# Another opening for a two-layer transformer kernel: norm weights in PSUM, a written order for the first token tiles, transpositions in idle time

## The chip, the cores and the metric

The kernel runs on one core of a Trainium2 chip. A core has TensorE (matrix products, into PSUM; PE in the profile), VectorE (DVE), ScalarE (ACT), GpSimd (POOL) and SyncE (SP, which issues most transfers). The engines run side by side; each works through its own list of instructions in order and waits on semaphores for the others. The metric is the time of one execution on the device in microseconds (us), lower is better; several executions are taken and their median is given.

## What is computed

A trunk of two layers over 1024 tokens of width 1024, all in float32: differential attention in the first, latent attention in the second, a gated MLP with a short convolution behind each. The change lies in the first steps of the first layer:

```python
def rms_norm(x, g):
    y = x * lax.rsqrt(jnp.mean(x * x, axis=-1, keepdims=True) + NORM_EPS)
    return y * g

h = rms_norm(x, attn_norm_g[0])
qkv = h @ w_qkv                      # 1024 x 3072: 8 heads, each 128 columns of q, k and v
q, k, v = jnp.split(qkv, 3, axis=-1) # then a partial rotary embedding of q and k
```

## The kernel before

**Tokens and heads.** The 1024 tokens are eight tiles of 128 rows; tiles 0 to 3 are half 0, tiles 4 to 7 half 1. A product on TensorE wants the features on the partitions, so each normalized tile is transposed ("turned") by eight 128x128 products with the identity matrix `ident`, four into each of two PSUM banks of 512 columns. Every product of the model is done in three: a float32 number is split into a high part (rounded to the format that TensorE takes at full rate, float32r) and a low part (the rest), and `mm3` adds high x low, high x high and low x high. ACT writes high parts (`hi`, line 141, CAST in the profile), DVE or POOL low parts (`lo`, line 144).

**A token tile** (`token_tile`): ACT squares the tile and sums (`squares`, line 171), DVE scales the sum (176), POOL takes the power -1/2 (177), DVE multiplies the tile by the root and by the norm weights `g` (328), TensorE turns it (196), ACT and DVE split it into `H`. The norm weights are loaded once with each row repeated on all 128 partitions (`gain`, line 203, a tile of 512 KB in s11).

**A unit** (`da_unit`) is one projection of one head for one half: (head, which, half) with which 0 for q, 1 for k, 2 for v. It is 24 products of 512 columns into PSUM bank `u`, of which there is one. For q and k the rotary embedding follows (`rope`: DVE 247 and 248 read the bank, POOL 249 and 250 combine), then ACT, DVE or POOL write the parts. For v, ACT copies the bank, and the result is turned. PSUM has two double banks `S`, three banks `b` and one `u`; names are handed out in rotation, and whoever gets one waits until its last reader is done.

**Order.** Code is written once for all engines. Unless a manual schedule is open, a scheduler in the framework orders each engine's list by its own estimate of times; inside `manual_schedule` the order of the code stands. The first part of `diff_attention` (lines 340 to 360) is left to the scheduler: weights of head 0 are fetched and split (`fetch_w`, `split_w`; the raw weights have two places in turn), tiles 0 to 3, unit (0,1,0), unit (0,0,0), tiles 4 to 7, unit (0,2,0). After that the loop over heads is played from a list (`DA_ORDER`), which neither kernel changes; it begins with scores of head 0 and unit (0,1,1). In the profile's names the letter is the kind of place: s, u and h are SBUF pieces of 2048, 1024 and 512 columns when they are 128 rows of data, and `b`, `u` and `S` written by TensorE are PSUM.

## Time and profile before

| | us |
|---|---|
| runs: 3, median | 2438.91 |
| lowest, highest | 2438.78, 2440.64 |
| the profiled execution's own time | 2438.93 |
| its span, first to last instruction | 2437.1 |

The profiled execution's time is 1.83 us more than its span, for what lies around the first and last instruction. How to read the lines below: a row of the order of time has the start and the length in us, engine, line of the kernel, operation, tile written <- tiles read, and in square brackets how long the engine had been idle and what ended that. A row that groups instructions has their number, busy time in us, mean of one in ns. A row of a window has its bounds, its length, the busy time (with number of instructions) of TensorE, its weight loads, DVE, ACT and POOL, the granted TensorE clock (1.00 is full), the share of the DMA engines and GB/s. Ends of products are modelled: two that follow each other overlap, so the distance of starts is what one costs.

### The profile page before, as it was taken

To read this page: it belongs to the slowest core of one execution; us is meant where nothing else is said; L and a number is where in the kernel's file an instruction comes from. 1 tells how busy PE (TensorE), PEld (TensorE's weight loads), DVE (VectorE), ACT (ScalarE), POOL (GpSimd) and SP (SyncE) were. 2 spreads that over 40 slices of the span, in tenths; PEclk is the share of its full clock that TensorE was granted. 3 is DMA by queue.
4 is the path that set the end of the run, shared out by engine and by line. 5 is a ranking of instruction groups with operands and counts; after the bars stand their busy time and mean duration, and the time that the engine had idled before them with its cause. 6 is when DMAs were issued, how large, how long until landed. Compare 5 with 4: busy or idle time off the path is not lost.

```text
span 2437.1 us, 32476 instructions
## 1 busy us (share of the span) xinstructions
PE 2361.4 (97%) x11864; PEld 1995.5 (82%) x11864; DVE 1916.4 (79%) x3108; ACT 1299.4 (53%) x2417; POOL 639.8 (26%) x502
## 2 busy tenths in 40 slices
PE   7999999899999999999999999999989999999998
PEld 5888888777888888878889888888878888887886
DVE  6577777847988888899965888886488888888997
ACT  5677777845444444444444777775354444443443
POOL 5555544525100000000042566655340000000001
PEclk9999999999999999999999999999999999999999
DMA  4111111313222222554231211124222222227501
GB/s 153 43 47 36 35 36 44 130 57 114 78 93 80 78 87 79 185 181 134 68 104 52 77 49 31 49 63 130 91 87 87 79 93 80 78 87 276 173 1 78
DMA packets 95135, 214.68 MB, mean 88 GB/s; under 512 B 8640, under 2 KB 33856, under 8 KB 94784
## 3 DMA queue, kind: packets, MB, share of 16 engines
q1 hardware_dynamic: 86080, 185.35, 22.9%
q10 hardware_dynamic: 8896, 27.27, 3.0%
q8 instruction: 93, 1.52, 0.3%
q14 instruction: 66, 0.54, 0.1%
HBM read 160.15 MB, written 52.43 MB: 87 GB/s over the span
## 4 chain that ended last, share of the span: by engine, by line
PE 75%; DVE 10%; ACT 5%; DMA 3%; issue 3%; POOL 3%; SPq 0%; POOLq 0%; ACTq 0%; DVEq 0%
PE S L133 12%; PE S L135 12%; PE S L134 12%; PE b L135 8%; PE b L134 8%; PE b L133 8%; PE u L133 3%; PE u L134 3%; PE u L135 3%; PE b L259 3%; DVE s L144 2%; ACT u L141 1%; PE u L1572 1%; PE u L1571 1%; POOL s L144 1%
## 5 line engine op out<-in xcount | busy, mean ns | idle before, releaser
L177 POOL TENSOR_TENSOR st<-st,mhalf 128x1 f32<-128x1 f32 x56 | 33.9, 606 | 1327.5 <-DVE st L176 1327.5
L141 ACT CAST u<-h 128x512 fp32r<-128x512 f32 (+1 forms) x242 | 145.9, 619 | 296.1 <-DVE h L669 263.5
L133 PE MATMUL S<-s,u 128*128 128x512 f32 (+1 forms) x752 | 286.5, 381 | 7.7 <-DVE s L144 5.6
L135 PE MATMUL S<-s,u 128*128 128x512 f32 (+1 forms) x752 | 285.2, 379 | 0.0
L134 PE MATMUL S<-s,u 128*128 128x512 f32 (+1 forms) x752 | 285.1, 379 | 0.0
L133 PE MATMUL b<-s,u 128*128 128x512 f32 x588 | 230.5, 392 | 1.2 <-ACT u L141 1.2
L135 PE MATMUL b<-s,u 128*128 128x512 f32 x588 | 229.6, 391 | 0.0
L134 PE MATMUL b<-s,u 128*128 128x512 f32 x588 | 229.3, 390 | 0.0
L717 DVE SCALAR_TENSOR_TENSOR u<-u,conv,u 128x1023 f32<-128x1023 f32 (+1 forms) x176 | 224.7, 1277 | 1.4 <-ACT u L713 1.4
L163 POOL TENSOR_TENSOR u<-u,st 128x384 f32<-128x384 f32 (+7 forms) x160 | 170.9, 1080 | 156.4 <-DVE st L1555 92.8
L133 PE MATMUL u<-s,s 128*128 128x512 f32 x448 | 181.4, 405 | 9.4 <-DVE h L248 6.9
L141 ACT CAST s<-u 128x512 fp32r<-128x512 f32 (+2 forms) x204 | 131.7, 682 | 105.9 <-PE u L135 34.7
L144 DVE TENSOR_TENSOR u<-b,u 128x512 fp32r<-128x512 f32 (+1 forms) x256 | 157.4, 629 | 27.0 <-ACT u L141 25.8
L135 PE MATMUL u<-s,s 128*128 128x512 f32 x448 | 176.7, 394 | 0.0
L134 PE MATMUL u<-s,s 128*128 128x512 f32 x448 | 176.4, 394 | 0.0
L133 PEld LDWEIGHTS S<-s,u 128*128 128x128 f32 x752 | 142.5, 189 | 36.4 <-DVE s L144 6.4
L134 PEld LDWEIGHTS S<-s,u 128*128 128x128 f32 x752 | 142.6, 190 | 26.3
L135 PEld LDWEIGHTS S<-s,u 128*128 128x128 f32 x752 | 142.5, 190 | 26.1
L720 ACT ACTIVATE u<-u 128x1024 f32<-128x1024 f32 x44 | 46.7, 1062 | 195.8 <-DVE u L717 195.8
L141 ACT CAST u<-b 128x512 fp32r<-128x512 f32 (+1 forms) x256 | 133.6, 549 | 25.7 <-PE b L259 13.0
L141 ACT CAST s<-h 128x512 fp32r<-128x512 f32 x144 | 86.6, 619 | 111.7 <-DVE h L900 51.0
L144 DVE TENSOR_TENSOR s<-u,s 128x512 fp32r<-128x512 f32 (+1 forms) x182 | 129.1, 743 | 10.4 <-ACT s L141 10.3
(261 smaller groups left out, 6617.4 us busy)
## 6 DMA issues: line engine op xcount, KB each, us to landing
u<-in_ffn_up SPq DMA_DIRECT2D x88, 512.0 KB, 3.6
g_d<-u ACTq DMA_DIRECT2D x44, 512.0 KB, 2.6
u<-in_ffn_down SPq DMA_DIRECT2D x66, 256.0 KB, 5.3
u<-g_d SPq DMA_DIRECT2D x62, 256.0 KB, 4.6
s<-in_da_wqkv SPq DMA_DIRECT2D x24, 512.0 KB, 3.7
x_d<-u SPq DMA_DIRECT2D x16, 512.0 KB, 2.6
s<-x_d SPq DMA_DIRECT2D x8, 1024.0 KB, 8.9
u<-o_d SPq DMA_DIRECT2D x24, 256.0 KB, 2.8
```

Of the source, the lines that this page charges most:

```text
L133: mm(out, lh, rl, start=first, stop=False, skip_group_check=onto)
L134: mm(out, lh, rh, start=False, stop=False, skip_group_check=onto)
L135: mm(out, ll, rh, start=False, stop=last, skip_group_check=onto)
L141: self.nc.scalar.copy(out, src)
L144: (eng or self.nc.vector).tensor_sub(out, src, hi.bitcast(F32))
L163: self.nc.gpsimd.tensor_mul(x, x, s.to_broadcast(list(x.shape)))
L177: nc.gpsimd.tensor_tensor(r, s, self.mhalf, ALU.pow)
L259: self.nc.tensor.transpose(ps[:, j * P : (j + 1) * P], probs[t][:, k : k + P], self.ident)
L717: nc.vector.scalar_tensor_tensor(t[half][:, back:], u[half][:, : S - back], w, t[half][:, back:], ALU.mult, ALU.add)
L720: nc.scalar.activation(t[0], t[0], AF.Silu)
L1571: nc.tensor.matmul(o[:, c0:], v, al, start=kb == 0, stop=False)
L1572: nc.tensor.matmul(o[:, c0:], v, ah, start=False, stop=kb == 2 * p + 1)
```

## The change

It has five parts, all before the loop over heads.

1. **Norm weights** (`gain_bank`). Instead of 128 repeated rows, 8 rows of 128 numbers are loaded (4 KB). TensorE turns them into a 128x8 column block, DVE widens each column to 128 equal columns (in s11), and TensorE turns these eight blocks into a double bank S, which then holds the weights on every partition. The tiles' norms read them from there; the bank is held until tile 7 is normalized.
2. **A written order** for tiles 0 to 3 on TensorE, DVE, ACT and POOL (`first_tiles`), and for TensorE alone up to the end of the products of unit (0,2,0). The scaling of the sum of squares moves from DVE to POOL for tiles 0 to 4. The squares' output, which nobody reads, goes to u13 instead of a double bank S.
3. **Idle transpositions** (`fill`): 5, 6, 14, 3, 4 and 10 products with `ident` whose results are overwritten, each group ahead of work that waits for another engine.
4. **The first unit's high products first** (`late`): eight high x high, then eight low x high, then eight high x low, so that the low parts are wanted last.
5. **Places**: unit (0,0,0) accumulates in a bank b; tile 4 is turned ahead of it, tile 5 behind it, tile 6 in the middle of unit (0,2,0), tile 7 behind its products. Tiles x0 to x4 are fetched at the start, x5 to x7 at once when their places are free; the fetches of head 1's weights and of the constants are written later.

```diff
+    def gain_bank(self, place, rows, src):
+        rows, wide = self.at(rows, [KD, P]), self.at(place, [P, KD, P])
+        self.nc.sync.dma_start(rows, src.rearrange("(k p) -> k p", p=P))
+        def make():
+            ps = self.bank("u")
+            self.fill(ps, self.ident, 5)
+            self.nc.tensor.transpose(ps[:, :KD], rows, self.ident[:KD, :KD])
+            self.nc.vector.tensor_copy(wide, ps[:, :KD].unsqueeze(2).to_broadcast([P, KD, P]))
+            g = self.big()
+            self.fill(g, self.ident, 6)
+            for k in range(KD):
+                self.nc.tensor.transpose(g[:, k * P : (k + 1) * P], wide[:, k, :], self.ident)
+            return g
+        return make
+
+    def fill(self, ps, src, n):
+        for _ in range(n):
+            self.nc.tensor.transpose(ps[:, :P], src[:, :P], self.ident)
...
-            r = self.rstd(x, self.big(), D)
+            r = r4 if i == 4 else self.rstd(x, junk, D)
...
-        xs = [fetch_x(0)]
-        g = self.gain("s11", a["attn_norm_g"][0])
-        xs += [fetch_x(1), fetch_x(2)]
+        def first_tiles():
+            E = mybir.EngineType
+            order = self.tc.manual_schedule(engines={E.PE, E.DVE, E.Activation, E.Pool})
+            order.__enter__()
...
+            def root(i):
+                s[i] = self.squares(xs[i], junk)
+                r[i] = self.stat()
+                nc.gpsimd.tensor_scalar(s[i], s[i], 1.0 / D, EPS, ALU.mult, ALU.add)
+                nc.gpsimd.tensor_tensor(r[i], s[i], self.mhalf, ALU.pow)
+
+            def norm(i):
+                nc.vector.scalar_tensor_tensor(xs[i], xs[i], r[i], g, ALU.mult, ALU.mult)
+
+            def turn(i, banks, n):
+                self.fill(banks[0], xs[i - 1] if i else self.ident, n)
+                for kg, ps in enumerate(banks):
+                    for k in range(4):
+                        b = kg * 512 + k * P
+                        nc.tensor.transpose(ps[:, k * P : (k + 1) * P], xs[i][:, b : b + P], self.ident)
...
+            g = gain()
+            for i in range(3):
+                root(i)
+                norm(i)
+            turn(0, (self.bank(), self.bank()), 14)
+            high(0)
+            root(3)
+            turn(1, (self.bank(), self.bank("u")), 3)
+            high(1)
+            low(0)
+            norm(3)
+            for b in (slice(0, 512), slice(512, D)):
+                self.hi(w[:, 0, b], raw[:, b])
+            for b in (slice(0, 512), slice(512, D)):
+                self.lo(w[:, 1, b], raw[:, b], w[:, 0, b], nc.gpsimd)
+            turn(2, both(self.big()), 4)
+            high(2)
+            low(1)
+            low(2)
+            turn(3, (self.bank(), self.bank()), 10)
+            high(3)
+            root(4)
+            low(3)
+            order.__exit__(None, None, None)
+            return g, r[4]
+
+        gain = self.gain_bank("s11", "h4", a["attn_norm_g"][0])
+        xs = [fetch_x(i) for i in range(4)]
+        junk = self.at("u13", [P, D])
         fetch_w(0, 1)
-        xs += [fetch_x(3)]
+        xs += [fetch_x(4)]
+        g, r4 = first_tiles()
+        nc.sync.dma_start(tab, a["rope_da"])
         fetch_w(0, 0)
-        nc.sync.dma_start(tab, a["rope_da"])
-        split_w(0, 1)
-        for i in range(4):
-            token_tile(i, xs[i])
-            if i == 1:
-                self.load_constants()
-        xs += [fetch_x(4), fetch_x(5), fetch_x(6)]
+        xs += [fetch_x(5), fetch_x(6), fetch_x(7)]
         fetch_w(0, 2)
+        order = self.tc.manual_schedule(engines={mybir.EngineType.PE})
+        order.__enter__()
         split_w(0, 0)
-        self.run([unit(0, 1, 0)])
+        self.run([unit(0, 1, 0, True)])
+        token_tile(4, xs[4])
+        self.run([unit(0, 0, 0, False, "b")])
+        token_tile(5, xs[5])
         split_w(0, 2)
+        last = [unit(0, 2, 0)]
+        self.run(last, 2)
+        token_tile(6, xs[6])
+        self.run(last, 1)
+        token_tile(7, xs[7])
+        order.__exit__(None, None, None)
+        self.run(last)
         fetch_w(1, 1)
-        self.run([unit(0, 0, 0)])
-        for i in range(4, NT):
-            if i + 3 < NT:
-                xs += [fetch_x(i + 3)]
-            token_tile(i, xs[i])
-        self.run([unit(0, 2, 0)])
+        self.load_constants()
...
-    def da_unit(self, R, H, W, which, half, hd, tab):
+    def da_unit(self, R, H, W, which, half, hd, tab, late=False, bank="u"):
...
+            if late:
+                nc.tensor.matmul(acc, part(0, k), tok(0, k), start=k == 0, stop=False)
+                continue
...
+        for w, p in ((1, 0), (0, 1)) if late else ():
+            for k in range(KD):
+                nc.tensor.matmul(acc, part(w, k), tok(p, k), start=False, stop=p == 1 and k == KD - 1)
```

What stands in the engines' lists. TensorE before, from its first instruction (`b` and `u` on the left of the arrow are banks, u_59 to u_63 tiles x0 to x3; L196 is the turn of a tile, L133 to L135 the three products of `mm3`):

```order
L196 MATMUL b_178<-ident,u_59_155 128x128 x4
L196 MATMUL b_185<-ident,u_59_155 128x128 x4
L196 MATMUL b_199<-ident,u_61_159 128x128 x4
L196 MATMUL b_206<-ident,u_61_159 128x128 x4
L196 MATMUL b_235<-ident,u_62_161 128x128 x4
L196 MATMUL b_242<-ident,u_62_161 128x128 x4
L196 MATMUL b_256<-ident,u_63_164 128x128 x4
L196 MATMUL b_263<-ident,u_63_164 128x128 x4
L133 MATMUL u_280<-s_49_141,s_64_168 128x512
L134 MATMUL u_280<-s_45_137,s_64_168 128x512
L135 MATMUL u_280<-s_45_137,s_64_168 128x512
```

TensorE now, from the turn of tile 1 on (L226 is `fill`, L382 the turn of a tile, L519 and L526 the first unit; u_62 to u_64 are x1 to x3, s_45 and s_46 the high parts of half 0):

```order
L226 MATMUL b_245<-ident,u_61_158 128x128 x3
L382 MATMUL b_245<-ident,u_62_160 128x128 x4
L382 MATMUL u_246<-ident,u_62_160 128x128 x4
L226 MATMUL S_267<-ident,u_62_160 128x128 x4
L382 MATMUL S_267<-ident,u_63_162 128x128 x8
L226 MATMUL b_286<-ident,u_63_162 128x128 x10
L382 MATMUL b_286<-ident,u_64_164 128x128 x4
L382 MATMUL b_287<-ident,u_64_164 128x128 x4
L519 MATMUL u_330<-s_45_137,s_67_172 128x512 x4
L519 MATMUL u_330<-s_46_138,s_67_172 128x512 x4
L526 MATMUL u_330<-s_45_137,s_67_172 128x512 x4
L526 MATMUL u_330<-s_46_138,s_67_172 128x512 x4
```

Behind each tile's turn there is now a group of fills for the next tile's bank, and the first unit begins with eight products that need high parts only. ACT before, from its third instruction on (L171 squares, L141 high parts; s_64 and s_91 are weights):

```order
L171 ACTIVATE S_192,st_71_193<-u_61_159 128x1024
L141 CAST s_45_137<-b_178 128x4x128
L171 ACTIVATE S_228,st_79_229<-u_62_161 128x1024
L141 CAST s_46_138<-b_185 128x4x128
L141 CAST s_64_168<-s_54_146 128x1024
L141 CAST s_45_137<-b_199 128x4x128
L171 ACTIVATE S_249,st_84_250<-u_63_164 128x1024
L141 CAST s_46_138<-b_206 128x4x128
L141 CAST s_91_277<-s_54_146 128x1024
```

ACT now, from its third instruction on:

```order
L171 ACTIVATE u_65_166,st_72_202<-u_62_160 128x1024
L171 ACTIVATE u_65_166,st_74_208<-u_63_162 128x1024
L141 CAST s_45_137<-b_214 128x4x128
L141 CAST s_46_138<-b_215 128x4x128
L171 ACTIVATE u_65_166,st_78_240<-u_64_164 128x1024
L141 CAST s_45_137<-b_245 128x4x128
L141 CAST s_46_138<-u_246 128x4x128
L141 CAST s_67_172<-s_54_146 128x512 x2
L141 CAST s_45_137<-S_267 128x4x128
L141 CAST s_46_138<-S_267 128x4x128
L141 CAST s_45_137<-b_286 128x4x128
L141 CAST s_46_138<-b_287 128x4x128
```

Three squares now come first, the fourth ahead of tile 1's high parts, and the weights' high part (in two halves) behind these. POOL before, from the fourth tile's root on (L177 is a root, L249 and L250 the rope, s_91, s_96 and s_126 low parts of weights):

```order
L177 TENSOR_TENSOR st_85_252<-st_84_250,mhalf 128x1
L144 TENSOR_TENSOR s_91_277<-s_54_146,s_91_277 128x1024
L177 TENSOR_TENSOR st_104_363<-st_103_361,mhalf 128x1
L177 TENSOR_TENSOR st_109_384<-st_108_382,mhalf 128x1
L177 TENSOR_TENSOR st_114_405<-st_113_403,mhalf 128x1
L144 TENSOR_TENSOR s_96_316<-s_54_146,s_96_316 128x1024
L177 TENSOR_TENSOR st_119_426<-st_118_424,mhalf 128x1
L249 TENSOR_TENSOR h_94_306<-h_94_306,s_53_145 128x512
L250 TENSOR_TENSOR h_93_305<-h_93_305,h_94_306 128x512
L144 TENSOR_TENSOR s_126_479<-s_54_146,s_126_479 128x1024
L249 TENSOR_TENSOR h_99_346<-h_99_346,s_53_145 128x512
L250 TENSOR_TENSOR h_98_345<-h_98_345,h_99_346 128x512
```

POOL now, over the same work (L270 and L271 are the rope, s_90 the query weights, s_105 the value weights, s_121 head 1's key weights):

```order
L144 TENSOR_TENSOR s_90_327<-s_54_146,s_90_327 128x1024
L177 TENSOR_TENSOR st_102_421<-st_101_419,mhalf 128x1
L270 TENSOR_TENSOR h_93_356<-h_93_356,s_53_145 128x512
L177 TENSOR_TENSOR st_108_457<-st_107_455,mhalf 128x1
L271 TENSOR_TENSOR h_92_355<-h_92_355,h_93_356 128x512
L144 TENSOR_TENSOR s_105_439<-s_54_146,s_105_439 128x1024
L177 TENSOR_TENSOR st_112_483<-st_111_481,mhalf 128x1
L144 TENSOR_TENSOR s_121_534<-s_54_146,s_121_534 128x1024
L270 TENSOR_TENSOR h_99_407<-h_99_407,s_53_145 128x512
L271 TENSOR_TENSOR h_98_406<-h_98_406,h_99_407 128x512
```

The rope of k now stands ahead of the low part of the value weights, and both that and the low part of head 1's key weights stand ahead of the rope of q, where before only the latter did. On SP the fetch of the 8 rows is first, then x0 to x3, key weights, x4, the rotary table, query weights, lambda, constants, x5 to x7, value weights, head 1's key weights.

More of the change, by code (lines that the diff above doesn't have):

```diff
@@ L419 @@
     )
-    def da_unit(self, R, H, W, which, half, hd, tab):
+    def da_unit(self, R, H, W, which, half, hd, tab, late=False, bank="u"):
         nc = self.nc
-        acc = self.bank("u")
+        acc = self.bank(bank)
+        part = lambda w, k: W[w][:, k * P : (k + 1) * P]
+        tok = lambda p, k: H[p][half][k // 4][:, k % 4, :]
         for k in range(KD):
-            wh, wl = (w[:, k * P : (k + 1) * P] for w in W)
-            rh, rl = (H[part][half][k // 4][:, k % 4, :] for part in range(2))
-            self.mm3(acc, wh, wl, rh, rl, k == 0, k == KD - 1)
+            if late:
+                nc.tensor.matmul(acc, part(0, k), tok(0, k), start=k == 0, stop=False)
+                continue
+            self.mm3(acc, part(0, k), part(1, k), tok(0, k), tok(1, k), k == 0, k == KD - 1)
             if k in (1, 3, 5):
                 yield
+        for w, p in ((1, 0), (0, 1)) if late else ():
+            for k in range(KD):
+                nc.tensor.matmul(acc, part(w, k), tok(p, k), start=False, stop=p == 1 and k == KD - 1)
         if which == 2:
```

18 lines of the change are left out of this document (16 added, 2 removed).

## The prediction

> **What bounds the kernel now.** I read the page first, then the start in order of time, then the clock.
>
> ```profile
> PE 2361.4 (97%) x11864; PEld 1995.5 (82%) x11864; DVE 1916.4 (79%) x3108; ACT 1299.4 (53%) x2417; POOL 639.8 (26%) x502
> PE 75%; DVE 10%; ACT 5%; DMA 3%; issue 3%; POOL 3%; SPq 0%; POOLq 0%; ACTq 0%; DVEq 0%
> ```
>
> TensorE is busy 97% of the span and three quarters of the chain that ended last; the edit touches only the first 50 us, so the question is how early TensorE gets through them. The stage in order of time (all engines up to 24 us, TensorE alone below):
>
> ```profile
> 0.73 0.38 SPq L323 DMA_DIRECT2D u<-in_x  x1
> 1.17 0.42 SPq L203 DMA_DIRECT2D s<-in_attn_norm_g  x1
> 4.56 1.03 ACT L171 ACTIVATE S<-u 128x1024 f32<-128x1024 f32 x1 [2.55 <-DMA u<-in_x]
> 5.74 0.15 DVE L176 TENSOR_SCALAR st<-st 128x1 f32<-128x1 f32 x1 [3.25 <-ACT S L171]
> 6.05 0.56 POOL L177 TENSOR_TENSOR st<-st,mhalf 128x1 f32<-128x1 f32 x1 [2.49 <-DVE st L176]
> 6.64 1.28 DVE L328 SCALAR_TENSOR_TENSOR u<-u,st,s 128x1024 f32<-128x1024 f32 x1 [0.75 <-POOL st L177]
> 7.66 1.03 ACT L171 ACTIVATE S<-u 128x1024 f32<-128x1024 f32 x1 [1.94 <-DMA u<-in_x]
> 7.98 1.97 PE L196 MATMUL b<-ident,u 128*128 128x128 f32 x8 [7.98 <-DVE u L328]
> ...
> 12.27 2.35 POOL L144 TENSOR_TENSOR s<-s,s 128x1024 fp32r<-128x1024 f32 x1
> 12.27 3.43 DVE L328 SCALAR_TENSOR_TENSOR u<-u,st,s 128x1024 f32<-128x1024 f32 x1
> ...
> 23.01 0.80 PE L133 MATMUL u<-s,s 128*128 128x512 f32 x1 [0.55 <-DVE s L144]
> 23.60 0.63 PE L134 MATMUL u<-s,s 128*128 128x512 f32 x1
> 24.02 0.63 PE L135 MATMUL u<-s,s 128*128 128x512 f32 x1
> ...
> 30.05 0.39 PE L134 MATMUL u<-s,s 128*128 128x512 f32 x1
> 30.28 0.39 PE L135 MATMUL u<-s,s 128*128 128x512 f32 x1
> ...
> 33.73 0.50 PE L133 MATMUL u<-s,s 128*128 128x512 f32 x1 [1.75 <-DVE h L248]
> 39.33 1.47 PE L196 MATMUL b<-ident,u 128*128 128x128 f32 x12
> 41.89 0.47 PE L133 MATMUL u<-s,s 128*128 128x512 f32 x1 [1.09 <-DVE h L248]
> 49.62 0.48 PE L133 MATMUL u<-s,s 128*128 128x512 f32 x1
> ```
>
> Three losses are to be seen. The first unit starts at 23.01 although tile 0 was normalized at 7.92: the norms of tiles 2 and 3 wait behind POOL (at 12.27 both operands of DVE lie in SBUF, as POOL's do, and DVE took 3.43 us for 1.28). The first products are 0.425 us apart (24.02 less 23.60), later ones 0.23 (30.28 less 30.05). And units two and three wait 1.75 and 1.09 us until rope has read their one bank u. From 49.62 on the rows of every engine are in the same order in both kernels within a few places, so I count up to that product, the first of key unit (0,1,1).
>
> **The change, step by step.** *Arrivals.* x0 is now issued behind 8 rows, 0.44 us later (1.17 less 0.73): it lands at about 4.95 (4.56 plus 0.4, rounded). Two transfers of 512 KB lie between 4.56 and 7.66, 1.55 us each; with the gain's gone, x1, x2, x3 land at 6.5, 8.1, 9.65, key weights at 11.2, x4 at 12.75. Behind them SP has the 1 MB table, query weights, lambda and constants, x5 to x7 and value weights: by the same step x5 lands at 19.4, value weights at 23.9. x5 waits on SP for tile 0's turn, done by 10.5, which is earlier than its place in the transfers.
>
> ```profile
> o_d<-h SPq DMA_DIRECT2D x16, 256.0 KB, 2.2
> s<-in_da_wqkv SPq DMA_DIRECT2D x24, 512.0 KB, 3.7
> ```
>
> *Gain.* No row shows a 4 KB transfer; between 2.2 us (above) and x0's 3.8 I take the nearer, 2.2: landed at 2.9. A transposition costs 0.2 us at the slow clock (1.97 for 8, with the drain), 0.11 fast (1.47 for 12). The copy that widens it reads PSUM, a form without a row; the adds below give 1.2, with ends 0.7 (half its width, second row) and 1.28. So 2.9, one transposition, copy to 4.6, eight transpositions: gain in PSUM at 6.4. In the bad case (3.8) at 8.0, which would set tile 0 back by 0.8.
>
> ```profile
> L494 DVE TENSOR_TENSOR u<-u,S 128x1024 f32<-128x1024 f32 x8 | 9.8, 1220 | 24.9 <-PE S L135 24.9
> L144 DVE TENSOR_TENSOR s<-b,s 128x512 fp32r<-128x512 f32 x16 | 10.4, 680 | 4.6 <-ACT s L141 4.5
> L141 ACT CAST s<-b 128x512 fp32r<-128x512 f32 x16 | 8.9, 588 | 11.7 <-PE b L196 11.6
> L171 ACT ACTIVATION_READ_ACCUMULATOR S<-u 128x1 f32 x8 | 1.5, 190 | 0.0
> L214 POOL MEMSET mhalf<- 128x1 f32 x1 | 0.1, 98 | 0.0
> ```
>
> *Roots.* TENSOR_SCALAR moves from DVE (0.15) to POOL. No row has it there: between 0.10 (MEMSET of the same shape) and 0.56 (the power) I take 0.3, so square to root is 1.05 us, against 0.92 before (5.72 to 6.64). *Norms* read the gain from PSUM: 1.22 as in L494 at best, 3.43 if POOL still held them up; POOL does only roots until 13 us, so I take 1.25. Tile 0 is normalized 7.2 to 8.5, tile 1 8.75 to 10.0, tile 2 10.3 to 11.6.
>
> *ACT* now sets the pace. A square with its read (1.03 and 0.19, which overlap) takes 1.06 to 1.2, casts in a row 0.5 to 0.55. Squares 0 to 2 end at 9.2; tile 0 is turned behind 14 fills (6.2 to 9.0), its high part is cast from 10.0 to 11.15; square 3 ends 12.2, tile 1's part 13.25, key weights 14.25, tile 2's 15.3. Tile 3: root 13.25, norm 14.55, turned 15.6, cast 15.3 to 16.4. The first unit needs only its first half, 15.85: it starts at 15.95 instead of 23.01, **7.05 us** earlier. The weights' low part (POOL, two halves of 1.3, from 2.35 for the whole at 12.27) ends 16.4 and tile 3's low part (DVE) by 18.3, before the products that need them at 17.8 and 19.6. DVE's small lambda operations stand ahead of norm 4 and cost nothing while their transfer lands by 18.
>
> *Clock.* The slow products last from 23.01 to about 27.1 (windows below), nine or so; if the fills have raised the clock by then, nine times 0.2 is **1.8 us**. *Banks.* Query unit in bank b, value unit behind tile 5: the waits of 1.75 and 1.09 go, **2.85 us**. The fills are hidden: TensorE waits for ACT or DVE there; if the clock stays slow they are not (below).
>
> *Given back.* The first unit ends at 21.55, the query unit, behind tile 4, at 27.95, tile 5's turn 28.85 (its norm, after root 5 at 21.5, is five us ahead). POOL has in order: low part of query weights, root 5, rope of k, root 6, low part of value weights (to 28.95), root 7, low part of key weights of head 1 (to 32.0), then rope of q. DVE's last scaling of k waits for POOL's lock until 32.0; tile 5's first low part follows (33.3), and tile 6's second turn needs that bank: TensorE stands from 32.1 to 33.35. The value unit ends 36.55, tile 7's turn 37.45.
>
> ```profile
> 43.78 2.55 ACT L141 CAST u<-h 64x512 fp32r<-64x512 f32 x4 [2.25 <-POOL h L250]
> 44.48 2.64 POOL L144 TENSOR_TENSOR h<-h,u 64x512 fp32r<-64x512 f32 x2 [0.73 <-ACT u L141]
> ```
>
> The q chain: POOL rope 32.65 to 35.2 (two of 1.28), casts to 37.75, low parts to 38.55 (3.34 after the casts begin, as 43.78 to 47.12). The last scores wait for these; unit (0,1,1) starts at 39.25. Of the tail 1.3 to 1.4 is given back: 7.05 + 1.8 + 2.85 - 1.35 = **10.35 us** (49.62 less 39.25 is 10.37). Moving the constants' load costs nothing: lambda is wanted at the first softmax, 20 us later. The squares' output goes to SBUF (u13), free until the first probabilities are turned.
>
> After that every load waits for a buffer, none for a time, so the lead should last. Against the profiled execution's own 2438.93 us (median of the runs 2438.91): 2438.93 - 10.35 = 2428.6.
>
> **The clock.** By window of 3.41 us, TensorE busy and granted clock; the second block is of operations with ident alone, that is transpositions.
>
> ```profile
> 20.32:23.73 3.41, 2.66 (x10) 2.20 (x11) 3.27 (x12) 1.99 (x4) 0.00 (x0) 1.00 1.03 414
> 23.73:27.14 3.41, 3.41 (x10) 2.67 (x9) 1.73 (x5) 3.41 (x8) 1.10 (x2) 1.00 0.08 30
> 474.29:477.70 3.41, 2.82 (x11) 2.66 (x12) 3.36 (x8) 2.44 (x6) 2.09 (x3) 0.50 0.37 107
> 1351.52:1354.93 3.41, 1.51 (x5) 0.97 (x6) 1.83 (x2) 3.34 (x7) 2.24 (x1) 1.00 0.39 148
> 1354.93:1358.34 3.41, 3.41 (x11) 2.78 (x10) 3.08 (x7) 1.42 (x4) 2.11 (x3) 0.50 0.49 154
> 1672.37:1675.78 3.41, 2.65 (x22) 2.32 (x21) 2.40 (x6) 3.36 (x7) 2.84 (x3) 1.00 0.00 0
> 1675.78:1679.19 3.41, 3.33 (x26) 3.16 (x27) 3.30 (x11) 2.52 (x8) 3.38 (x3) 1.00 0.45 115
> ```
>
> ```profile
> 1351.52:1354.93 3.41, 0.00 (x0) 0.00 (x0) 0.00 (x0) 0.00 (x0) 1.00 0.39 148
> 1672.37:1675.78 3.41, 1.28 (x10) 1.07 (x10) 0.00 (x0) 0.00 (x0) 1.00 0.00 0
> ```
>
> 1.51 busy dropped the clock for the next window. 2.65, of which 1.37 were products and 1.28 transpositions, did not: transpositions count in holding the clock. A full window raised it, 2.82 did not; whether a full window of transpositions raises it, no row tells. (The rows before 27 us say 1.00, but 0.425 per product shows half.) The fills make TensorE busy without a gap from about 4.6 to 14 us, so a full window ends by 11.5 wherever windows lie.
>
> The Trainium skill (TensorE: Matmul & The Clock Gate, Part 4) says that the full clock "doesn't engage for transpose-mode". By that rule the first unit would run slow, and the sum would be the first rival's. For holding the clock the rows at 1672 disagree; for raising it they are silent.
>
> **Rivals.** *Fills that don't raise the clock.* They then stand in the way, 0.2 each: tile 1's turn ends 12.75, tile 2's 15.1, ten fills 17.1, tile 3's 18.7, the unit starts 18.7 (2.75 later), runs nine products slow (1.8) and ends 25.95; the query unit ends 32.4, the value unit with three turns 40.6, and with scores and a turn, some 1.5, (0,1,1) starts at 42.1, lead 7.5: 2431.4. For it: the silence above. Against: 1672.
>
> *The clock's windows later on.* It fell at 1354.93 and 474.29 after idle stretches; such a fall costs half the busy time at half clock, 1.7 (3.41/2) to 3.1 where two windows ran slow (2.82 plus 3.41, halved). A shift of the work may add one or save one: 2431 or 2425.5. Three windows are 10.24 us, nearly my shift, so that I expect the falls at the same work.
>
> *No change.* The weights of key unit (0,1,1)'s head (head 1) are loaded when POOL has let go of their buffer, 20.95, and land at about 25.3; both ACT (ahead of scaling k) and POOL (ahead of rope of q) have them in hand order. Landing after 28.4 delays q one for one; from 33.9 on (28.4 plus 10.35 less 4.9) less than 0.2% is left, 2439 at 38.8.
>
> *Slower,* by the same wait: from a landing at 43.6 (another 9.8) the kernel is past 2443.8, at 46 it takes 2446.2. Against both: 24 such loads took 3.7 us from issue.
>
> **How the numbers follow.** The likeliest, 2427 to 2430 around 2428.6: 0.62. Fills without the clock (2431.4): 0.16. Windows otherwise: 0.14, half each way. No change: 0.04; slower: 0.04. With 0.56 for the root on POOL nothing moves, ACT being later; with 3.8 for the rows 0.8 is lost; with no stand at tile 6, 1.2 won. The range 2425.5 to 2433 takes in both clock cases with these (2431.4 plus 0.8 and some): about 0.88 by the cases, less for what I have missed. 0.2% is 4.9 us, about what a measurement of this kernel can tell; faster by more 0.92, within 0.04, slower 0.04.
>
> **What would show it.** Tile 0's norm ends near 8.5; products of the first unit begin near 16 and are 0.23 apart from the first; no wait on rope between units; a wait of about 1 us at tile 6's turn; unit (0,1,1) near 39.3; every later group unchanged. I am wrong if the first unit runs at 0.425, if q's rope on POOL starts long after 33, or if the lead at 50 us isn't there at 500.

## The result and the profile after

| | before | after |
|---|---|---|
| median of the runs, us | 2438.56 (6 runs, 2436.94 to 2440.64) | 2429.89 (6 runs, 2428.97 to 2431.9) |
| profiled execution: time, span | 2438.93, 2437.1 | 2429.01, 2427.2 |

The ratio is 0.9965 (95% interval 0.9952 to 0.9978): 8.67 us by the medians, 9.92 by the two profiled executions; 10.35 was forecast. Executions of one kernel lie 2 to 6 us apart; that the windows in which the clock is granted fall otherwise in each of them is one reason that the traces below show.

First the page of the changed kernel, its busy times and its chain that ended last:

```profile
PE 2362.9 (97%) x11915; PEld 1997.0 (82%) x11915; DVE 1912.6 (79%) x3104; ACT 1300.2 (54%) x2418; POOL 640.8 (26%) x508
PE 75%; DVE 11%; ACT 5%; DMA 3%; issue 3%; POOL 2%; SPq 0%; POOLq 0%; ACTq 0%; DVEq 0%
```

The shares are within one per cent of those before; TensorE ran 51 instructions more (42 fills and the nine transpositions of the norm weights). The change is to be seen in the order of time only. TensorE up to the first product of unit (0,1,1), and one product further on:

```profile
2.00 1.33 PE L226 MATMUL u<-ident 128*128 128x128 f32 x5 [2.00 <-POOL ident masks.py:199]
...
8.60 1.09 PE L382 MATMUL b<-ident,u 128*128 128x128 f32 x8
...
14.34 1.09 PE L382 MATMUL b<-ident,u 128*128 128x128 f32 x8 [0.20 <-DVE u L375]
15.67 2.11 PE L519 MATMUL u<-s,s 128*128 128x512 f32 x8 [0.24 <-ACT s L141]
17.62 3.79 PE L526 MATMUL u<-s,s 128*128 128x512 f32 x16
21.25 1.03 PE L196 MATMUL b<-ident,u 128*128 128x128 f32 x8
22.04 0.48 PE L133 MATMUL b<-s,s 128*128 128x512 f32 x1
...
31.24 0.60 PE L196 MATMUL b<-ident,u 128*128 128x128 f32 x4
33.39 0.66 PE L196 MATMUL b<-ident,u 128*128 128x128 f32 x4 [1.55 <-DVE s L144]
...
39.45 0.50 PE L133 MATMUL u<-s,s 128*128 128x512 f32 x1
...
53.12 0.50 PE L133 MATMUL u<-s,s 128*128 128x512 f32 x1 [0.81 <-ACT h L529]
```

The first unit starts at 15.67 (23.01 before), its sixteen later products take 3.79 us, 0.24 each (0.425 for the first nine before), the query unit follows a turn without a wait, and unit (0,1,1) starts at 39.45 instead of 49.62: a lead of 10.17. Between these two starts the only stand left (a stretch in which TensorE waits for another engine) is 1.55 us ahead of tile 6's second turn. VectorE in the same kernel, with the norms of tiles 4 and 6, and what GpSimd did meanwhile:

```profile
18.12 1.27 DVE L349 SCALAR_TENSOR_TENSOR u<-u,st,S 128x1024 f32<-128x1024 f32 x1
...
25.16 1.28 DVE L349 SCALAR_TENSOR_TENSOR u<-u,st,S 128x1024 f32<-128x1024 f32 x1
...
30.68 1.93 DVE L543 SCALAR_TENSOR_TENSOR u<-h,u 64x512 fp32r<-64x512 f32 x1
```

```profile
18.17 2.41 POOL L144 TENSOR_TENSOR s<-s,s 128x1024 fp32r<-128x1024 f32 x1
...
29.68 2.39 POOL L144 TENSOR_TENSOR s<-s,s 128x1024 fp32r<-128x1024 f32 x1
```

The norm at 18.12, whose weights lie in PSUM (S), ran in 1.27 us beside a low part on GpSimd; the scaling of k at 30.68, whose operands both lie in SBUF (h, u), took 1.93 for half of its work. What this difference is worth is measured below: 2.4 us by itself, and together with the load of 512 KB nearly the whole gain.

### The profile page after: what moved, and what is told of

The parts are those of the page before. It is cut to its first block, busy times and chain, and to the rows that moved or that the text cites. A ratio compares the mean times of both kernels' runs of the same rounds, so it can differ in the third digit from the quotient of the medians.

```text
span 2427.2 us, 32582 instructions
## 1 busy us (share of the span) xinstructions
PE 2362.9 (97%) x11915; PEld 1997.0 (82%) x11915; DVE 1912.6 (79%) x3104; ACT 1300.2 (54%) x2418; POOL 640.8 (26%) x508
## 4 chain that ended last, share of the span: by engine, by line
PE 75%; DVE 11%; ACT 5%; DMA 3%; issue 3%; POOL 2%; SPq 0%; POOLq 0%; ACTq 0%; DVEq 0%
PE S L133 12%; PE S L135 12%; PE S L134 12%; PE b L135 8%; PE b L134 8%; PE b L133 8%; PE u L133 3%; PE b L280 3%; PE u L134 3%; PE u L135 3%; DVE s L144 2%; ACT u L141 2%; PE u L1668 1%; PE u L1667 1%; DMA s<-in_da_wqkv 1%
## 5 line engine op out<-in xcount | busy, mean ns | idle before, releaser
L177 POOL TENSOR_TENSOR st<-st,mhalf 128x1 f32<-128x1 f32 x51 | 31.6, 622 | 1313.1 <-DVE st L176 1313.0
L141 ACT CAST u<-h 128x512 fp32r<-128x512 f32 (+1 forms) x242 | 145.9, 619 | 294.3 <-DVE h L765 263.4
L133 PE MATMUL S<-s,u 128*128 128x512 f32 (+1 forms) x752 | 286.0, 380 | 7.8 <-DVE s L144 5.6
L135 PE MATMUL S<-s,u 128*128 128x512 f32 (+1 forms) x752 | 284.7, 379 | 0.0
L133 PE MATMUL b<-s,u 128*128 128x512 f32 x588 | 230.3, 392 | 1.6 <-ACT u L141 1.6
L135 PE MATMUL b<-s,u 128*128 128x512 f32 x588 | 229.1, 390 | 0.0
L141 ACT CAST s<-u 128x512 fp32r<-128x512 f32 (+2 forms) x205 | 132.3, 681 | 105.2 <-PE u L135 34.5
L133 PE MATMUL u<-s,s 128*128 128x512 f32 x432 | 173.6, 402 | 6.1 <-DVE h L269 3.9
L133 PEld LDWEIGHTS S<-s,u 128*128 128x128 f32 x752 | 141.9, 189 | 36.6 <-DVE s L144 6.7
L135 PE MATMUL u<-s,s 128*128 128x512 f32 x432 | 169.4, 392 | 0.0
L134 PE MATMUL u<-s,s 128*128 128x512 f32 x432 | 169.3, 392 | 0.0
L135 PEld LDWEIGHTS S<-s,u 128*128 128x128 f32 x752 | 141.9, 189 | 26.3
L141 ACT CAST s<-h 128x512 fp32r<-128x512 f32 x144 | 86.6, 619 | 113.1 <-DVE h L996 52.3
L141 ACT CAST u<-b 128x512 fp32r<-128x512 f32 (+1 forms) x256 | 133.6, 549 | 24.3 <-PE b L280 13.1
```

What stands on the lines that cost most here:

```text
L133: mm(out, lh, rl, start=first, stop=False, skip_group_check=onto)
L134: mm(out, lh, rh, start=False, stop=False, skip_group_check=onto)
L135: mm(out, ll, rh, start=False, stop=last, skip_group_check=onto)
L141: self.nc.scalar.copy(out, src)
L177: nc.gpsimd.tensor_tensor(r, s, self.mhalf, ALU.pow)
```

## The experiments

The last product shown above, the one that waits for ScalarE's copy of a value unit's bank (line 529), is in every kernel: it starts at 63.26 before and at 53.12 after, 10.14 earlier. It is the mark below; "lost" is how much later than 53.12 it came. The same opening, run twice, came 0.92 apart there (52.87 and 51.95, the run with q's rope first and the run of both orders), so less than 1 us is read as nothing. This rests on one pair, and each mark is that of one profiled execution; the medians count beside it. One reason for the spread shows in the traces: lambda's small load, whose operations stand ahead of tile 4's norm on VectorE. In the run with q's rope first VectorE waited 0.89 us for it and the norm started at 19.93; in the other it had landed and the norm started at 17.63.

| run | mark | lost | median, us | ratio (95%) |
|---|---|---|---|---|
| the change | 53.12 | 0 | 2429.89 | 0.9965 (0.9952 to 0.9978) |
| no idle transpositions | 53.25 | 0.13 | 2430.44 | 0.9968 (0.9955 to 0.998) |
| scheduler's order for tiles 0 to 3 | 53.71 | 0.59 | 2428.71 | 0.9957 (0.9943 to 0.9971) |
| first unit in triples | 56.13 | 3.01 | 2433.56 | 0.9974 (0.9965 to 0.9984) |
| the same, ten transpositions more | 56.32 | 3.20 | 2433.61 | 0.9976 (0.9967 to 0.9986) |
| query unit in bank u | 59.16 | 6.04 | 2433.69 | 0.9977 (0.9968 to 0.9986) |
| no transpositions, triples, bank u | 61.21 | 8.09 | 2436.93 | 0.9995 (0.9986 to 1.0005) |
| 512 KB of norm weights, in SBUF | 62.44 | 9.32 | 2438.22 | 0.9997 (0.9987 to 1.0006) |
| 8 rows, then in SBUF | 55.50 | 2.38 | 2431.85 | 0.9974 (0.9965 to 0.9983) |
| 512 KB, then in PSUM | 55.74 | 2.62 | 2433.04 | 0.9976 (0.9966 to 0.9985) |
| q's rope first on GpSimd | 52.87 | -0.25 | 2428.96 | 0.9959 (0.9947 to 0.9972) |
| the same, query unit in bank u | 57.92 | 4.80 | 2433.93 | 0.9981 (0.9972 to 0.999) |
| q's rope first, down additions first | 51.95 | -1.17 | 2424.62 | 0.9941 (0.9929 to 0.9954) |

Two theories stood against each other. A: the chain on GpSimd and VectorE that ends in q's rope sets when unit (0,1,1) starts, so that TensorE's parts are worth little alone. B: each term of the sum counts in full. Both fell: unit (0,1,1), which starts at 39.45 in the changed kernel, came at 39.58 without the fills (A had 40.0 to 41.0, B 42.0 or later), at 42.49 with triples and at 44.19 with bank u, which is later than either theory had it.

### The idle transpositions

```diff
     def fill(self, ps, src, n):
-        for _ in range(n):
-            self.nc.tensor.transpose(ps[:, :P], src[:, :P], self.ident)
+        return
```

> The changed kernel with all 42 idle transpositions left out; the marker is the start of the first product of unit (0,1,1), 39.45 us in the changed kernel. Theory A (up to the marker the chain DVE/POOL that ends in the rope of q decides, TensorE has slack ahead of it): the clock rises only in the first full window of products, so about half of the first unit runs at 0.425 us per product, the key unit ends near 23.9 instead of 21.2, but the marker moves by only 0.5 to 1.5, to 40.0 to 41.0. Theory B (the sum of the prediction, every term in full): the fills are worth the slow products and the slow turns, marker at 42.0 or later. If idle transpositions do not raise the clock at all, nothing changes: marker 39.4 and the clock's first rise at the same time.

TensorE of this run at the turn of tile 0 and half of tile 1, and at the first unit:

```profile
8.50 2.82 PE L381 MATMUL b<-ident,u 128*128 128x128 f32 x12 [2.73 <-DVE u L374]
...
15.81 2.11 PE L518 MATMUL u<-s,s 128*128 128x512 f32 x8 [0.24 <-ACT s L141]
17.75 3.79 PE L525 MATMUL u<-s,s 128*128 128x512 f32 x16
```

These are turned at the slow clock (2.82 us for twelve, 0.235 each), and yet the first unit runs at 0.24 per product from 15.81: the turns of tiles 0 to 2, useful transpositions now close together, had raised the clock by 12.2. With the fills it rose at 7.39. In both kernels TensorE did nothing but transpose in the window before. These two windows by operations with ident alone, first the changed kernel, then the one without fills (TensorE busy 3.41 of 3.41):

```profile
3.98:7.39 3.41, 3.41 (x17) 3.16 (x16) 0.00 (x0) 0.00 (x0) 1.00 0.92 353
...
8.79:12.20 3.41, 3.41 (x18) 3.26 (x17) 0.00 (x0) 0.00 (x0) 1.00 1.04 431
```

So transpositions alone raise the clock. The Trainium skill (TensorE: Matmul & The Clock Gate, Part 4) has it that the full clock does not engage for transpose mode; this case's runs disagree, if its transpositions are in that mode, which the trace does not say (it calls them MATMUL). But ScalarE and VectorE set the pace up to 15.7, and the earlier rise is worth nothing here. In these executions the clock's 1.8 us came from the turns' being close together and did not need the fills. That the window of 8.79 began just behind the turns' start, at 8.50, was luck: the only other profile without fills has its window at 8.64, behind a start at 8.59, and what a later window would do is not shown.

### Triples, bank u, and all three parts out

```diff
-        self.run([unit(0, 1, 0, True)])
+        self.run([unit(0, 1, 0)])
```

> The changed kernel with the first unit's products in threes again (high x low first), so that it waits for tile 3's low part on DVE. Both: first product near 17.25 instead of 15.67, key unit ends near 22.8 instead of 21.2. Theory A: marker moves by 0 to 0.6, to at most 40.1. Theory B: marker moves by the whole 1.5, to 41.0.

```diff
-        self.run([unit(0, 0, 0, False, "b")])
+        self.run([unit(0, 0, 0)])
```

> The changed kernel with unit (0,0,0) back in the one bank u, so that its first product waits for the rope of k. Both theories: it starts near 23.9 instead of 22.0, and the value unit waits for the rope of q. Theory A: the rope of q on POOL starts no later than before (POOL is behind with low parts until 32), marker at 39.4 to 40.2. Theory B: the two waits of 1.75 and 1.09 us are back in full, marker at 41.5 to 42.3.

Triples: the first triple already wants a low part of tile 3, so the unit starts at 17.12, 1.45 later. TensorE at tile 6's second turn, and the two clock windows around it (busy time of TensorE first, the granted clock third from the end):

```profile
35.49 0.82 PE L196 MATMUL b<-ident,u 128*128 128x128 f32 x4 [2.24 <-DVE s L144]
...
36.54 0.63 PE L134 MATMUL u<-s,s 128*128 128x512 f32 x1
36.96 0.63 PE L135 MATMUL u<-s,s 128*128 128x512 f32 x1
```

```profile
32.45:35.86 3.41, 1.17 (x9) 0.84 (x8) 3.35 (x4) 0.59 (x1) 3.32 (x3) 1.00 0.45 154
35.86:39.27 3.41, 3.41 (x11) 2.74 (x10) 1.11 (x3) 2.95 (x5) 2.55 (x2) 0.50 0.01 2
```

The stand is 2.24 us instead of 1.55; TensorE was busy 1.17 us of a window, and the next ran at half clock, products 0.425 apart: half of its 3.41 us is lost, 1.7. In the changed kernel the window at the same place had 1.86 busy and the clock held:

```profile
31.28:34.69 3.41, 1.86 (x13) 1.49 (x12) 3.38 (x4) 1.17 (x2) 3.33 (x3) 1.00 0.47 155
```

Bank u, TensorE of that run at the query and value units, and its clock:

```profile
25.27 0.47 PE L133 MATMUL u<-s,s 128*128 128x512 f32 x1 [2.48 <-ACT s L141]
...
33.99 0.76 PE L133 MATMUL u<-s,s 128*128 128x512 f32 x1 [2.12 <-DVE h L269]
```

```profile
30.52:33.93 3.41, 1.36 (x11) 0.99 (x9) 3.35 (x7) 1.07 (x2) 3.41 (x3) 1.00 0.51 154
33.93:37.34 3.41, 3.35 (x8) 2.70 (x9) 1.11 (x2) 1.16 (x2) 2.60 (x3) 0.50 0.45 154
```

The waits that were 1.75 and 1.09 us in the old kernel are 2.48 and 2.12: with the unit done by 21.5 the rope is late on VectorE, behind the norms of tiles 4 and 5. The second one again drops the clock. 4.6 of waits and some 1.5 of clock, less the stand of 1.55 that is gone, make unit (0,1,1) 4.74 later (44.19); the rest of the 6.04 comes behind it, with waits of 0.51 and 1.36 at 52.06 and 59.16. Part of the price is this execution's: VectorE waited 0.72 us for lambda's load, and lambda's next operation, both of whose operands lie in SBUF, took 1.84 instead of 0.21 beside a low part on GpSimd (17.98 to 20.37), so that tile 4's norm started 2.25 later than in the changed kernel:

```profile
18.60 1.84 DVE L254 TENSOR_TENSOR h<-h 128x64 f32<-128x64 f32 x1
20.37 1.27 DVE L349 SCALAR_TENSOR_TENSOR u<-u,st,S 128x1024 f32<-128x1024 f32 x1
```

The medians are only 3.80 us apart. The triples run had the same late load (norm of tile 4 at 20.36), and so had the one without fills (20.70), where it cost nothing at the mark; the run of the three edits together did not (18.33). How much of 6.04 and 3.01 is due to it is not measured.

The two edits and the one without idle transpositions, together:

> Three parts taken out at once: no idle transpositions, the first unit in triples, the query unit in bank u. Left are the norm weights from 8 rows, the hand order and the later loads. One at a time these cost 0.13, 2.98 and 6.02 us at 77 us (10.14 with all). Theory 'each part counts in full': they add up, 9.1, and the lead is 1.0. Theory 'they stand in the same row': a later end of the first unit is hidden by the query unit's wait for bank u, which VectorE's row ends at about 25.3 whether the unit ends at 21.5 or 22.8, and the falls of the clock behind the stands are one and the same: the loss is that of bank u alone, lead 3.5 to 4.2.

This run (the three edits together) lost 8.09; the single losses sum to 9.18, and bank u alone cost 6.04. So neither plain sum (a lead of 1.0 was expected by it) nor full overlap (3.5 to 4.2) holds. Here, without fills, TensorE was busy 1.58 us of the window from 15.47 to 18.88, and the clock fell in the first unit too. Whether the missing fills did this is not shown: with fills, the same wait of the first unit dropped the clock in one execution and not in another (see "Does a stand cost twice?"). What is left of the change, the weights in PSUM and the hand order, leads by 2.05 at the mark and does not show in the time.

### The norm weights: transfer or place

```diff
-            g = gain()
+            self.fill(self.bank("u"), self.ident, 20)
+            g = wide
...
-        gain = self.gain_bank("s11", "h4", a["attn_norm_g"][0])
-        xs = [fetch_x(i) for i in range(4)]
+        xs = [fetch_x(0)]
+        wide = self.gain("u14", a["attn_norm_g"][0])
+        xs += [fetch_x(i) for i in range(1, 4)]
```

> The norm weights come as in the old kernel, as one transfer of 512 KB repeated on all partitions, asked for behind the first token tile, into SBUF; the two banks, the eight small transpositions and the widening copy fall away, 20 idle transpositions are kept so that the clock rises alike. Term 'weights from 8 rows': at the rate of the first 20 us (about 400 GB/s) 512 KB are 1.3 us, so token tiles 1 to 4 land 1.3 us later. If the transfers set the pace, the first unit starts at 16.9 instead of 15.67 and the lead at 77 us falls from 10.14 to about 8.9. Rival: ScalarE, which has squares and casts in a row, sets the pace, tiles land ahead of it, and the lead stays within 0.4 of 10.1.

This one edit lost 9.32 us, nearly the whole change; nothing of the kind was expected (leads of 8.9 or 10.1, measured 0.82). VectorE's norms of tiles 4 to 7, which now have both operands in SBUF (u), and its scaling of k; then GpSimd beside them, then TensorE:

```profile
20.60 3.47 DVE L349 SCALAR_TENSOR_TENSOR u<-u,st,u 128x1024 f32<-128x1024 f32 x1 [0.65 <-POOL st L372]
...
30.76 4.57 DVE L349 SCALAR_TENSOR_TENSOR u<-u,st,u 128x1024 f32<-128x1024 f32 x2 [0.38 <-POOL st L177]
35.36 3.47 DVE L545 SCALAR_TENSOR_TENSOR u<-h,u 64x512 fp32r<-64x512 f32 x2
```

```profile
20.59 2.40 POOL L144 TENSOR_TENSOR s<-s,s 128x1024 fp32r<-128x1024 f32 x1
...
31.21 6.35 POOL L144 TENSOR_TENSOR s<-s,s 128x1024 fp32r<-128x1024 f32 x2
```

```profile
18.09 2.11 PE L521 MATMUL u<-s,s 128*128 128x512 f32 x8 [0.24 <-ACT s L141]
...
34.30 0.50 PE L135 MATMUL u<-s,s 128*128 128x512 f32 x1 [2.25 <-POOL s L144]
40.25 1.97 PE L196 MATMUL b<-ident,u 128*128 128x128 f32 x8 [3.39 <-DVE h L269]
```

The first unit starts 2.42 later; then VectorE and GpSimd hold each other up (3.47 for a norm of 1.27, 6.35 for two low parts of 2.4), and TensorE stands 2.25 and 3.39, with the clock fallen in 11.96 to 15.37 and again behind 39.26. The Trainium skill (SBUF — State Buffer, "Who interferes with whom") says that a VectorE instruction with two inputs in SBUF contends with a GpSimd instruction that reads SBUF, and one with a single such input, outside its two-port modes, does not; the norms agree, 1.27 with the weights in PSUM and 3.47 with them in SBUF. The norms of tiles 0 to 3 took 1.28 here too (6.87 to 16.1), where the old kernel's tiles 2 and 3 had 3.43 and 3.36. GpSimd's low part of the weights starts only at 14.93, just behind the last of them (14.88): the order in time freed these, not the place. To part the load from the place, two halves were run. In the first the weights come from 8 rows and are copied to SBUF; in the second they come as 512 KB, as above, and are copied to PSUM.

```diff
-            return g
+            flat = self.at("u14", [P, D])
+            self.nc.vector.tensor_copy(flat, g)
+            return flat
```

> The norm weights are loaded and turned from 8 rows as in the changed kernel, but VectorE then copies them from the two banks to SBUF (one copy of about 1.2 us), and all norms read them there. With the 512 KB load the lead at 77 us was 0.82 instead of 10.14; that run changed two things, how much is loaded and where the norms read. Theory 'lock': what was lost is VectorE's norms of tiles 4 to 7, which read SBUF alone and stand while GpSimd's low parts run (3.47 us for one norm and 4.57 for two, instead of 1.27 each): the loss is here too, less the load's share; the copy delays tile 0 by 0.75, and the lead falls to 3 to 5. Theory 'load': what was lost is the 512 KB ahead of tiles 1 to 4: only the copy counts here, lead 9 or more.

```diff
-            g = gain()
+            self.fill(self.bank("u"), self.ident, 20)
+            root(0)
+            g = self.big()
+            nc.scalar.copy(g, wide)
```

> The other half: the 512 KB load as in the old kernel, but ScalarE copies the weights to the two banks (one copy of about 1.05 us, once they have landed at about 6.9), and the norms read the banks. Theory 'lock': the norms of tiles 4 to 7 take 1.27 us again; the load and the copy delay the first unit by 2 to 3.5 us, part of which the stand at tile 6's turn covers, lead 7 to 9. Theory 'load': lead 0.5 to 2, as with the load and SBUF.

TensorE of the first half (rows, then SBUF), with the stand that its tile 7 turn met, and of the second (512 KB, then PSUM), with the stand at tile 6:

```profile
16.28 2.11 PE L521 MATMUL u<-s,s 128*128 128x512 f32 x8 [0.24 <-ACT s L141]
...
38.81 1.26 PE L196 MATMUL b<-ident,u 128*128 128x128 f32 x8 [3.11 <-DVE s L144]
```

```profile
16.23 2.12 PE L524 MATMUL u<-s,s 128*128 128x512 f32 x8 [0.24 <-ACT s L141]
...
34.52 1.71 PE L196 MATMUL b<-ident,u 128*128 128x128 f32 x8 [2.16 <-DVE h L269]
```

Each half alone lost 2.4 to 2.6; together they lose 9.3. The place in SBUF makes a stand of 3.11 in place of 1.55; the load delays the unit by 0.56, makes one of 2.16 and drops the clock behind it (1.71 us for eight transpositions that take 1.03). The first half's lead, 7.76, lies between the theories "lock" (VectorE's norms held up by GpSimd, 3 to 5) and "load" (9 or more); the second's, 7.52, is what "lock" had for it (7 to 9). So some 4.3 of the 9.32 appear only when load and place come together, beside the falls of the clock. The traces show where they meet: ScalarE with the 512 KB in SBUF, then in the changed kernel (line 257 is the exponential of lambda, 171 the square of tile 5):

```profile
24.50 0.20 ACT L257 ACTIVATE st<-st 128x2 f32<-128x2 f32 x1 [3.98 <-DVE st L255]
24.61 1.04 ACT L171 ACTIVATE u<-u 128x1024 f32<-128x1024 f32 x1
```

```profile
19.29 1.06 ACT L171 ACTIVATE u<-u 128x1024 f32<-128x1024 f32 x1 [1.20 <-DMA u<-in_x]
...
20.35 0.19 ACT L257 ACTIVATE st<-st 128x2 f32<-128x2 f32 x1
```

In both runs with the load the scheduler has put the exponential ahead of the square, in the other two behind it. With the place in SBUF as well, the norm of 3.47 stands ahead of lambda's sums on VectorE, ScalarE waits 3.98 for them, and tile 5's square starts at 24.61, against 21.62 with the load alone, 19.45 with the place alone and 19.29 in the changed kernel. No run changes this order alone, so how much of the 4.3 it makes is not measured.

### The hand order and GpSimd's chain

The manual schedule of `first_tiles` is left out:

```diff
-            order = self.tc.manual_schedule(engines={E.PE, E.DVE, E.Activation, E.Pool})
-            order.__enter__()
...
-            order.__exit__(None, None, None)
```

> The hand order of the first tiles is left to the scheduler; all instructions stay. It puts the squares of tiles 0 to 3 and the cast of the key weights ahead of the first cast of tile 0 on ScalarE. If ScalarE's row sets the start, the first unit starts near 18.7 (3 us later) and the lead at 77 us falls to about 7.5. Rival: the order hardly matters because transfers set the pace: start within 0.5 of 15.67, lead 9.7 or more.

The start is at 17.68, 2.0 later (3 was expected, or under 0.5), and only 0.59 of it is left at the mark: there is no stand at tile 6 then (its eight transpositions at 33.22 in a row). The delay went into the stand of 1.55. That is no rule: with triples the unit started 1.45 later and the stand grew to 2.24. One difference is that the scheduler has tile 4's norm at 15.67, ahead of lambda's operations. GpSimd's rows around the later units were also ordered by hand, with roots 5 to 7 early and the low part of head 1's weights behind tile 7 (and so behind q's rope):

```diff
-        order = self.tc.manual_schedule(engines={mybir.EngineType.PE})
+        roots = {4: r4}
+        order = self.tc.manual_schedule(engines={mybir.EngineType.PE, mybir.EngineType.Pool})
...
+        roots[5] = self.rstd(xs[5], junk, D)
...
+        fetch_w(1, 1)
...
         token_tile(7, xs[7])
+        split_w(1, 1)
```

> The changed kernel with POOL's order written by hand too: the low part of head 1's key weights stands behind the whole rope and low parts of q instead of ahead of it. Theory A: the rope of q begins near 30 instead of 32.0, the wait of 1.55 us at tile 6's second turn shrinks to below 0.9, marker 37.5 to 38.4, total 1 to 2 us less than the changed kernel. Theory B (TensorE decides): only the wait at tile 6 shrinks, marker not below 38.8.

The same with the query unit in bank u:

> GpSimd's chain to q's rope shortened as in the run with q's rope first (which alone brought 0.24 us at 77 us), and the query unit back in bank u. Theory 'GpSimd's chain decides': with it shortened the query unit's wait for bank u is what is left, the lead falls by less than with GpSimd's old order, to 7 or 8. Theory 'TensorE's own row decides': the waits of 2.48 and 2.12 us for bank u come from VectorE's share of k's and q's rope (shuffle and products), not from GpSimd, and are there in full, with the clock's fall behind the second: lead 4.1 to 4.5.

The mark moved by 0.25, so q's rope on GpSimd does not set it: theory A falls. With bank u 4.80 is lost, with a wait of 3.05 at 25.47 and the clock fallen ahead of it (24.92). The lead is 5.34, between the two forecasts (7 to 8, and 4.1 to 4.5); as VectorE reads the bank for k's rope only at 24.04 to 25.3, behind the norms, the longer wait is VectorE's, not GpSimd's.

### Does a stand cost twice?

Triples again, with this ahead of tile 6's turn:

```diff
+        self.fill(self.big(), self.ident, 10)
         token_tile(6, xs[6])
```

> The run with the first unit in triples again (2433.56; the product that started at 53.12 in the changed kernel started at 56.13), with ten idle transpositions more, ahead of tile 6's first turn, where TensorE stands 2.24 us afterwards anyway. In that run TensorE was busy 1.17 of 3.41 us (32.45 to 35.86), and the clock fell to half in the next window, in which products are 0.43 apart. Theory 'a stand costs twice': the ten add 1.1 us of busy time to that window, 2.3, the clock holds, the stand shrinks to about 1.1 and ends at the same time, and the product starts 1.4 to 1.6 us earlier, at 54.5 to 54.7. Rival 'idle transpositions do not hold the clock': it falls at 35.9 as before, start 56.1; or, if they delay the turn itself, up to 57.2.

Three of its clock windows, two around the first unit and one at tile 6:

```profile
14.69:18.10 3.41, 1.51 (x9) 1.10 (x8) 3.06 (x6) 3.05 (x5) 1.94 (x4) 1.00 0.74 244
18.10:21.51 3.41, 3.41 (x10) 2.63 (x9) 2.63 (x5) 0.67 (x1) 2.08 (x1) 0.50 1.03 400
35.17:38.58 3.41, 1.98 (x14) 1.61 (x13) 2.58 (x3) 2.56 (x5) 2.61 (x3) 1.00 0.16 64
```

At tile 6 the clock held, with 1.98 busy, and the twelve products behind it took 2.86 us (37.65 to 40.51) against 4.38. The ten transpositions lie almost wholly in the window before (from 34.12); they moved tile 6's first turn, 0.60 us from 35.21, into this one, which without it would have had about 1.4 (an estimate: 1.98 less 0.60). As the windows lie otherwise than in the run with triples alone (32.45 to 35.86), this is no clean test of what held the clock. And in this execution it fell at 18.10, because of the unit's first wait of 1.90 us, which the other triples run has too. There, by its clock windows, the wait lies otherwise:

```profile
15.38:18.79 3.41, 1.67 (x7) 1.41 (x8) 2.73 (x7) 2.50 (x5) 2.12 (x4) 1.00 0.66 247
```

So after the same wait, 1.67 busy held the clock and 1.51 dropped it; which of them it is depends on where the windows lie in that execution. The mark came at 56.32, where the rival had it (54.5 to 54.7 was expected). The medians are the same (2433.61 and 2433.56), so that ten transpositions there buy nothing that can be measured.

### A version that beats both

The lead moves by 1 to 2 us later in the run, where windows fall to half clock (in the changed kernel two from 461.37 and one each from 597.90, 1027.98 and 2212.40). The last two follow stands in the feed-forward part, of 3.10 and 2.62 us; the old kernel's there are 1.66 and 1.88, and its clock held. Why they are longer now is not shown. VectorE and TensorE of the changed kernel there:

```profile
1024.86 1.29 DVE L996 TENSOR_TENSOR h<-u,u 128x512 f32<-128x512 f32 x2 [3.35 <-DMA u<-g_d]
1026.08 1.27 DVE L1130 TENSOR_TENSOR s<-s,b 128x512 f32<-128x512 f32 x2
```

```profile
1026.81 0.50 PE L133 MATMUL b<-s,s 128*128 128x512 f32 x1 [3.10 <-DVE s L1130]
```

VectorE waits 3.35 us for a load with a sum that nobody wants yet (996); the addition that frees TensorE's bank (1130) is queued behind it. The edit puts the additions first and one sum a tile later, and takes q's rope first along:

```diff
-            if t == 1:
-                sums(0)
-                high(0)
-            if t == 2:
-                sums(1)
...
                 nc.vector.tensor_add(x, x, y[b])
+            if t == 1:
+                sums(0)
+                high(0)
+            if t == 3:
+                sums(1)
```

> Two things on top of the changed kernel: GpSimd's row with q's rope ahead of the low parts (as run before: 2428.96), and, in both feed-forward parts, VectorE's additions of the down product ahead of the sums that wait for a load. In the changed kernel TensorE stands 3.10 us at 1026.81 and 2.62 at 2211.45 for such an addition, and the granted clock falls for 3.41 us behind each. If the stands are only this order, both go, and with them both falls (1.4 to 1.7 us each): 2420 to 2422. Rival: VectorE's row is as long as before and the stand comes back a few products later: 2427 to 2429.

VectorE no longer stands for that load, and TensorE's stands at these places are:

```profile
1030.68 0.50 PE L133 MATMUL b<-s,s 128*128 128x512 f32 x1 [1.47 <-DVE s L1131]
...
2213.02 0.50 PE L133 MATMUL b<-s,s 128*128 128x512 f32 x1 [0.96 <-DVE s L1131]
```

It takes 2424.62 us (ratio 0.9941, 0.9929 to 0.9954), 4.34 less than with q's rope first alone; 2420 to 2422 was expected. Stands of 1.47 and 0.96 stay, for the next such load, and another of 1.25 at 2225.46; neither drops the clock. From 711 to 1020 us of the old kernel the leads of this run and of the changed kernel over it are equal (12.5); behind the first of these places, at 1164, they are 13.2 and 10.9, and at the end 15.6 and 9.9.

## Why the prediction was right

Step by step, by its own terms.

- *First unit* at 15.95, measured 15.67. The root's scaling on GpSimd takes 0.19 us (between 0.10 and 0.56, 0.3 was taken); tile 0's square began at 5.07 (4.95 for its landing).
- *Clock*, 1.8 us: the products are 0.24 apart from the first, as forecast, and the rival in which transpositions do not raise the clock is out. The fills did raise it, at 7.39, but were not needed: without them it rose at 12.20, and the lead is the same.
- *Bank waits*, 2.85: gone, as forecast. The price was that of the old kernel's waits; at the new pace the waits in bank u are 4.6 with a fall of the clock behind them, 6.04 at the mark and 3.80 by the medians. The term is what the change gained over the old kernel, not what this part is worth in the new one.
- *Given back*, 1.35: the stand at tile 6 is there, 1.55 (31.84 to 33.39) where 1.25 was forecast, by the mechanism named, VectorE's scaling of k beside GpSimd's low part. The further sentence, that the last scores wait for q's rope, did not come true: the view shows no wait of TensorE between 33.39 and 39.45, and q's rope first on GpSimd moves nothing.
- *Norm weights in PSUM.* The sum weighed this for the first tiles alone (1.25 instead of 3.43), and there the place brings nothing: with the weights in SBUF they took 1.28. That norms 4 to 7 would otherwise stand beside the low parts was not priced; the run with 512 KB in SBUF shows that without this part hardly anything of the gain is left (0.82 at the mark).
- *Lambda's load* was to cost nothing if it landed by 18. It did, and VectorE used it at 17.92 without a wait; but in six of the other kernels' profiles VectorE had to wait for it until 18.27 to 18.89, and tile 4's norm started at 19.9 or later. That it was in time is luck.
- *The total.* At the mark the lead is 10.14 (10.35 forecast). At the end it is 9.92 in the profiled executions and 8.67 by the medians, a move of 0.4 to 1.7 where up to 3.1 was allowed. In the profiles the lead wanders by the clock's windows, the second rival. They were expected to fall at the same work: of the old kernel's falls from 464.05, 474.29, 607.41 and 1354.93, the second and third stayed, behind stands of 2.28 and 3.1 that both kernels have, the others went, and those from 1027.98 and 2212.40 are new. Six windows at half clock against five: that it nearly balanced is luck too. What makes the medians' 1.25 less is not shown, as the other executions left no order of time.

Why the sum came out although its parts do not add up: it summed the old kernel's losses, each read from its trace, as if all went at once, and all did go at once. This is a reading of the above; no run tests it.

## What to carry to other kernels

A sum over the losses in the trace of before prices the change as a whole; what each part is worth has to be measured in the new kernel, where slack of 1.5 us can hide one delay and two delays together can drop the clock. Where GpSimd works beside VectorE, ask of each VectorE instruction whether one of its operands can lie in PSUM. And a wait for a load belongs behind the work that frees TensorE's banks, not ahead of it.

## What the runs showed of the hardware

Transpositions with the identity alone raised the granted clock, at 7.39 us, after a window of 3.41 us filled with them. Of the windows looked at, those with up to 1.36 us busy of 3.41 (0.44, 0.92, 1.17, 1.36) were followed by one at half clock, those with 1.67, 1.86 and 1.98 were not. In between both are seen: 1.51, 1.58 and 1.66 (the last in the scheduler's order, from 1779.43) dropped it, 1.55 (512 KB in SBUF, from 32.44) and 1.57 (8 rows, then in SBUF, from 34.13) did not. Half of a window is about the bound, and the ends of products are modelled. A stand of 2 us therefore costs nothing more or up to 1.7 more by where the windows lie.

Of a VectorE and a GpSimd instruction whose operands all lie in SBUF, the one that started first kept its time in the rows above and the other waited. A low part on GpSimd from 20.59 took 2.40 and VectorE's norm from 20.60 took 3.47 (512 KB in SBUF); a norm from 18.72 took 1.29 and the low part from 18.77 took 3.49 instead of 2.41 (8 rows, then in SBUF). With the weights in PSUM both kept theirs: 1.27 from 18.12 and 2.41 from 18.17.
